# Hybrid encoder block on one core: the rotation of one query pair is moved behind that of the next one, and the key reads with it

## The chip, the core and the metric

The kernel runs on one core of a Trainium2 chip. A core has five engines that run their own instruction streams side by side: TensorE (PE; weight loads are listed apart as PEld), VectorE (DVE), ScalarE (ACT), GpSimd (POOL) and SyncE (SP), which here only issues DMA transfers. ScalarE also issues DMAs, and its DMA instructions stand in the same queue as its arithmetic. Work is handed from one engine to another through semaphores. The two on-chip memories are SBUF (128 partitions) and PSUM, into which matmuls write. The metric is the time of one execution in microseconds (us); less is better.

## The reference

Two inputs, 512 rows and 256 rows of width 2048, go through the same block; the kernel holds them together as 768 rows (`T`), kept transposed as columns. What matters here:

```
h = rmsnorm(x);  z = h @ w_in            # 1024 Fourier | 1024 q | 256 k | 256 v
of = fourier_mix(zf, w_fourier)          # Re(2-D DFT), per-group linear map
q, k = apply_rope(q), apply_rope(k)      # x*cos + rotate_half(x)*sin, head_dim 64
oa = window_attention(q, k, v, sink)     # 16 q heads, 4 kv heads, +-128 positions
x = x + concat(rmsnorm(of), rmsnorm(oa)) @ w_out
x = x + relu(rmsnorm(x) @ w_up)**2 @ w_down;  y = rmsnorm(x)
```

Everything is float32 at the interface. The kernel splits operands into a high part and a remainder in a shorter float format (`wh`/`wl`, `zh`/low part, `ofh`/`ofl`) and adds three products, so each matrix product is three matmuls, and each operand needs one ScalarE instruction (high) and one VectorE instruction (low).

## The kernel before

**Stages.** In order: the v projection, the Fourier columns of `w_in`, then the stage that this change is in: the q and k columns of `w_in` (L802), with the Fourier mix running between its matmuls; then attention together with the Fourier half of `w_out` (L848, L1040); the other half of `w_out`; the up projection; the down projection.

**The q/k stage.** It has 20 pieces (`for piece in range(n_in)`). Four pieces make one *pair*: 256 columns of `w_in`, two channel blocks `c` = 0, 1 of 128, against all 768 rows (two halves `s` of 384). Pair 0 is k; pairs 1 to 4 are the q groups 2, 0, 1 and 3 (`order`). One piece is 48 matmuls: first 24 for `c` = 0, then 24 for `c` = 1. A pair's four PSUM tiles (tag `ps`, four buffers, L802) are complete at the end of its fourth piece. They are then copied to SBUF (L815), block `c` = 0 in the middle of that piece and block `c` = 1 after it. The next pair's matmuls use the same four PSUM buffers, so its first matmul needs the copy of `c` = 0, `s` = 0, and so on.

**Weights.** Each piece's weights come by one 512 KB load into `raw` (two buffers, L79), then `wh` (ACT, L69) and `wl` (DVE, L70). The load of piece p+2 needs the `raw` buffer that piece p gives up when its `wl` is done. Pieces are split two ahead of their matmuls.

**Rotation of a pair.** Rotation works on the tile `zs` (128 x 2 x 768), in three steps of 256 columns: `cross` (POOL, L687: `zy` = the other block times sine), `turned` (DVE, L694 and L696: times cosine, then minus and plus `zy`), `parts` (ACT, L706 or L709: the high part `zh`; DVE, L707 or L710: the low part in place). Each step's parts are written to DRAM by two DMAs that ScalarE issues (L704, 256 KB each: `kh`, `kl` for keys, `qh`, `ql` for queries). Pairs 0 and 1 leave PSUM while the Fourier mix holds the space, so they are put into DRAM as they are and read back by `load_z` (SP, L678). Pairs 2 and 3 are copied from PSUM straight into a `zs` tile of the pool `zo`; pairs 0, 1 and 4 use a `zs` tile of the pool `kp`. Each pool has one buffer of that name. So the copy of pair 3 needs pair 2's writes to be finished, the read-back of pair 1 needs pair 0's, and the copy of pair 4 needs pair 1's.

**Reads for attention.** `load_k` (L720) reads the rotated keys, four DMAs of 768 KB into `kdh` and `kdl`. `load_q` (L731) reads one unit's queries into `qs`, a buffer shared with the `zh` tiles. `load_of` (L188) reads Fourier rows into `ofr`; the first of them use the two `zy` buffers.

**Order.** On TensorE the order is as written. In this stage the other engines' order comes from a scheduler that follows the program order, which the table in the `for pair, t, ahead in ...` loop sets: `after(t, fn)` puts a step behind the first half (t = n - 0.5) or the whole (t = n) of piece n. An engine executes its instructions strictly in that order, so one that waits holds up all behind it. From piece 19 on, the order of SP, ACT, DVE and POOL is as written too. In the attention stage the writing order comes from a list of times, counted in eighths of one output tile (`at(t, fn)`): `t_turn` and `t_parts` place the rotation of pair 4, the last one, `split_of(m)` the high and low parts of row tile m (`ofh`, `ofl`).

Of the kernel before, what the change touches and what calls it, by code (L numbers as in the profile page):

```python
# [11 lines left out]
F32 = mybir.dt.float32  # L12
# [8 lines left out]
P = 128  # L21
# [14 lines left out]
HALF = T // 2  # L36
# [4 lines left out]
def hybrid_encoder(ctx: ExitStack, tc: tile.TileContext, a: dict):  # L41
    nc = tc.nc
    ctx.enter_context(tc.manual_schedule(engines={mybir.EngineType.PE}))

    def f32(ap):
        return ap.bitcast(F32)
# [132 lines left out]
    def load_of(m, tiles=None):  # L179

        of_raw[m] = tiles or [
            op.tile([P, FG, P], F32, tag=f"of{'hl'[m - 1]}-1", name="ofr")
            if m < 3 else ap_.tile([P, FG, P], F32, tag="ofr", name="ofr", bufs=2)
        ]
        for i, raw in enumerate(of_raw[m]):
            k = raw.shape[1]
            src = of_d[i * k * P : (i + 1) * k * P, m * P : (m + 1) * P]
            nc.sync.dma_start(raw[:], src.rearrange("(k p) t -> p k t", p=P))  # L188
# [9 lines left out]
    with ExitStack() as ph:  # L198
# [456 lines left out]
        kt = {}  # L655
# [20 lines left out]
        def load_z(pair):  # L676
            z_tile(pair)
            nc.sync.dma_start(zt[pair][:], zs_d[pair][:].rearrange("(b p) t -> p b t", p=P))  # L678
# [3 lines left out]
        def cross(pair, s):  # L682

            ts = slice(s * 256, (s + 1) * 256)
            y = ys[pair, s] = kt["kp"].tile([P, 2, 256], F32, tag="zy", name="zy", bufs=2)
            for b in range(2):
                nc.gpsimd.tensor_tensor(out=y[:, b], in0=zt[pair][:, 1 - b, ts], in1=kt["sinr"][:, ts], op=ALU.mult)  # L687

        def turned(pair, s):

            ts = slice(s * 256, (s + 1) * 256)
            z, y = zt[pair][:, :, ts], ys.pop((pair, s))
            cb = kt["cosr"][:, ts].rearrange("p (o t) -> p o t", o=1).to_broadcast([P, 2, 256])
            nc.vector.tensor_tensor(out=z, in0=z, in1=cb, op=ALU.mult)  # L694
            for b, op in enumerate((ALU.subtract, ALU.add)):
                nc.vector.tensor_tensor(out=z[:, b], in0=z[:, b], in1=y[:, b], op=op)  # L696

        def parts(pair, s, when=lambda dt, fn: fn()):

            ts = slice(s * 256, (s + 1) * 256)  # L700
            z = zt[pair][:, :, ts]
            out, scale = (kr_d, None) if pair == 0 else (qr_d[order[pair]], HD ** -0.5)
            hi = kt["kp"].tile([P, 2, 256], F32R, tag="zy" if pair == len(cols) - 1 else "qs", name="zh", bufs=2)
            put = lambda o, x: nc.scalar.dma_start(out[o][:, ts].rearrange("(b p) t -> p b t", p=P), x)  # L704
            if scale is None:
                nc.scalar.activation(hi[:], z, AF.Copy)  # L706
                low = lambda: nc.vector.tensor_tensor(out=z.bitcast(F32R), in0=z, in1=f32(hi[:]), op=ALU.subtract)  # L707
            else:
                nc.scalar.activation(hi[:], z, AF.Copy, scale=scale)  # L709
                low = lambda: nc.vector.scalar_tensor_tensor(  # L710
                    out=z.bitcast(F32R), in0=z, scalar=scale, in1=f32(hi[:]), op0=ALU.mult, op1=ALU.subtract
                )
            put(0, f32(hi[:]))
            when(t_zl, low)
            when(t_zp, lambda: put(1, z))
# [9 lines left out]
        def load_q(u):  # L725
            b, g = units[u]
            t0 = slice(b * P, (b + 1) * P)
            qs = kt["kp"].tile([P, 4, P], F32R, tag="qs", name="qs", bufs=2)
            state[u] = {"qs": qs}
            for o in range(2):  # L730
                nc.sync.dma_start(f32(qs[o * HD : (o + 1) * HD]), qr_d[g][o][:, t0].rearrange("(d h) t -> d h t", h=4))  # L731
# [3 lines left out]
        def after(piece, fn):  # L735
            todo.setdefault(piece, []).append(fn)
# [10 lines left out]
        after(10, open_attention)  # L747
        cols = [2048, 1536, 1024, 1280, 1792]
        order = [None, 2, 0, 1, 3]
        for pair, t, ahead in ((0, 10.5, 10), (2, 11.5, None), (1, 13, 12), (3, 15, None)):  # L750
            if ahead is not None:
                after(ahead, lambda pair=pair: load_z(pair))
            for s in range(3):
                after(t + s // 2 * 0.5, lambda pair=pair, s=s: cross(pair, s))
                after(t + 0.5 + s // 2 * 0.5, lambda pair=pair, s=s: (turned(pair, s), parts(pair, s)))
        after(13, load_k)
        for u in range(2):
            after(17 + 0.5 * u, lambda u=u: load_q(u))
        after(17, lambda: load_of(0, [kt["kp"].tile([P, 4, P], F32, tag="zy", name="ofr", bufs=2) for _ in range(2)]))
        n_in = 4 * len(cols)  # L760
        in_raw, in_w = {}, {}

# [25 lines left out]
        for piece in range(n_in):  # L788
            pair, j = divmod(piece, 4)
            if piece == 19:  # L790
                last.enter_context(tc.manual_schedule(engines={mybir.EngineType.SP, mybir.EngineType.Activation, mybir.EngineType.DVE, mybir.EngineType.Pool}))
            if j == 0:
                ps = [[pp.tile([P, 512], F32, tag="ps", bufs=4, name="pz") for _ in range(2)] for _ in range(2)]
            piece_split(piece + 2)
            wh, wl = in_w.pop(piece)
            for c in range(2):
                cs = slice(c * P, (c + 1) * P)
                for i in range(4):
                    first, stop = j == 0 and i == 0, j == 3 and i == 3
                    for w, o, n in ((wh, 0, 0), (wh, 1, 1), (wl, 0, 2)):  # L800
                        for s in range(2):
                            nc.tensor.matmul(  # L802
                                ps[c][s][:, :HALF], w[:, i, cs], whole[j // 2][s][o][:, 4 * (j % 2) + i, :],
                                start=first and n == 0, stop=stop and n == 2,
                            )
                if j == 3:
                    if c == 0 and pair >= 2:
                        z_tile(pair)
                    if pair < 2:
                        zs = fp.tile([P, T], F32, tag="zs", name="zs", bufs=2)  # L810
                        put = [zs[:, :HALF], zs[:, HALF:]]
                    else:
                        put = [zt[pair][:, c, s * HALF : (s + 1) * HALF] for s in range(2)]
                    for s in range(2):
                        (nc.vector.tensor_copy if piece == n_in - 1 and c == 1 else nc.scalar.copy)(put[s], ps[c][s][:, :HALF])  # L815
                    if pair < 2:
                        nc.scalar.dma_start(zs_d[pair][c * P : (c + 1) * P, :], zs[:])
                    if piece == n_in - 1 and c == 0:
                        piece_split(piece + 3)
                if c == 0:  # L820
                    for fn in todo.pop(piece - 0.5, ()):
                        fn()
            for fn in todo.pop(piece, ()):
                fn()
# [159 lines left out]
    pace, t_first, t_qk, d_qk, t_max, t_exp, t_norm = 7.37, 4, -4.5, 1.73, 0.4, 2.65, 3.65  # L984
    t_trans, d_trans, t_th, t_tl, t_pv, d_pv, t_ob, t_os, t_put = 9.2, 1.05, 1.2, 1.4, 16.2, 0, 0.5, -0.6, 2.2
    t_w, t_of, t_xc, t_y, t_oa, t_oa0, t_oa1, t_lq = 42.05, 7.45, -0.05, 2.7, 67, 4.2, 4.95, 1.5
    t_cross, t_turn, t_parts = (0, 0.1, 3.2), (3, 4.6, 6.5), (5.9, 7.6, 9.5)
    t_sq, t_red, t_w3, d_w, t_of1, t_of2, t_lof, t_la = 6.7, 7.9, 1.65, 2.15, 3, 6.5, 15.2, 1
    events, clock = [], [0.0, 0]

    def at(t, fn):
        clock[1] += 1
        heapq.heappush(events, (t, clock[1], fn))
# [9 lines left out]
    for u in range(len(units)):  # L1003
        t = pace * u + t_first
        for h in range(4):
            dt = t_qk + d_qk * h
            at(t + dt, lambda u=u, h=h: qk(u, (h,)))
            at(t + dt + t_max, lambda u=u, h=h: row_max(u, (h,)))
            at(t + dt + t_exp, lambda u=u, h=h: exps(u, (h,)))
        at(t + t_norm, lambda u=u: normalize(u))  # L1010
        if u + 2 < len(units):
            at(t + t_lq + (u == 1), lambda u=u: load_q(u + 2))
        for kb in range(3):
            at(t + t_trans + d_trans * kb, lambda u=u, kb=kb: trans(u, kb))
            at(t + t_pv + d_pv * kb, lambda u=u, kb=kb: pv(u, kb))
# [43 lines left out]
    if True:  # L1059
# [3 lines left out]
        for n in range(4):  # L1063
            for m in range(NM):
                ps = pp3.tile([P, 512], F32, tag="mm", name="pm", bufs=2)
# [586 lines left out]
    ps = [pp.tile([P, 2, 512], F32, tag="ps", name="pd") for _ in range(3)]  # L1652
    ps = [x[:].rearrange("p a b -> p (a b)") for x in ps]
# [27 lines left out]
    for u, (kh, i, j) in enumerate(dunits):  # L1681
        if j == 0 and u > 0:
            ps = [pp.tile([P, 2, 512], F32, tag="ps", name="pd") for _ in range(3)]
            ps = [x[:].rearrange("p a b -> p (a b)") for x in ps]
# [121 lines left out]
```

## Time and profile before

| | |
|---|---|
| median of 3 runs | 2603.39 us (2602.78 to 2604.97) |
| the profiled execution | 2604.47 us |
| its span, first to last instruction | 2602.6 us |
| PE busy in the span | 2579.5 us |
| mean granted TensorE clock | 0.997 |

Stretches of the span, from the times at which the matmuls of a line begin and end: v projection to 57 us, Fourier columns to 173, q/k stage 173.4 to 389.2, attention with the first half of `w_out` from 389.2 to about 610, the rest after that. All times in the rows are from the start of the span. "Landing" of a DMA is the time from its issue to its semaphore. In the chain of waits each row is start, length, what. In a timeline the bracket at a row's end is the engine's idle time before the instruction and what ended it. Rows with PEq, ACTq or SPq are the engine's queue issuing a DMA or waiting.

### The profile page before, as it was taken

The numbers are of one execution on the slowest core, as the hardware profiler recorded it, in microseconds if no ns is written. First come the engines' busy times: TensorE is split into PE (matmuls) and PEld (weight loads), VectorE is DVE, ScalarE is ACT, GpSimd is POOL, SyncE is SP. The second block draws the span as 40 slices with busy tenths as digits, with TensorE's granted clock in tenths as the row PEclk, the third lists the DMA queues.
The fourth block names the chain that finished last, engine by engine and source line by source line (L and its number), as shares of the span: only waits on it lengthen the run. The fifth ranks groups of instructions, "written<-read, shape, count | busy, mean of one in ns | idle before, by whom it ended". The sixth has DMA issues, their size and how long they took to land.

```text
span 2602.6 us, 34971 instructions
## 1 busy us (share of the span) xinstructions
PE 2579.5 (99%) x13580; PEld 2360.6 (91%) x13580; DVE 1808.6 (69%) x2208; ACT 1124.5 (43%) x1574; POOL 264.9 (10%) x367
## 2 busy tenths in 40 slices
PE   9999989999999999999999999999999999999998
PEld 9999987888899999999999999988888888888887
DVE  7966548777556565555777787757776765777687
ACT  6545426675333334333544454433333333333335
POOL 1001323233210011000000000010000000000000
PEclk9999999999999999999999999999999999999999
DMA  7963375345664545466666766685553672554364
GB/s 253 312 221 119 119 217 184 116 127 181 211 207 157 174 162 174 152 206 239 205 213 214 233 232 211 222 319 177 178 164 111 209 244 79 176 183 158 97 210 156
DMA packets 268998, 489.54 MB, mean 188 GB/s; under 512 B 19568, under 2 KB 164000, under 8 KB 267424
## 3 DMA queue, kind: packets, MB, share of 16 engines
q1 hardware_dynamic: 197328, 321.26, 39.0%
q10 hardware_dynamic: 58688, 115.18, 11.7%
q0 software_dynamic: 12816, 50.87, 5.8%
q8 instruction: 107, 1.75, 0.3%
q14 instruction: 59, 0.48, 0.1%
HBM read 360.35 MB, written 126.88 MB: 187 GB/s over the span
## 4 chain that ended last, share of the span: by engine, by line
PE 95%; DVE 2%; DMA 1%; ACT 1%; issue 0%; POOL 0%; ACTq 0%; DVEq 0%; POOLq 0%; SPq 0%
PE pu L1187 35%; PE pd L1622 35%; PE pm L1040 10%; PE pz L802 5%; PE p L268 4%; PE pv L391 1%; PE o L924 1%; PE s L848 1%; PE t L905 1%; DMA raw<-in_w_in 1%; PE pe L630 0%; PE pa L609 0%; PE ptx L137 0%; DMA zs<-zs 0%; POOL zy L687 0%
## 5 line engine op out<-in xcount | busy, mean ns | idle before, releaser
L1187 PE MATMUL pu<-xf,wh 128*128 128x384 f32 x3072 | 780.2, 334 | 0.3
L1187 PEld LDWEIGHTS pu<-xf,wh 128*128 128x128 f32 x3072 | 553.8, 188 | 2.1 <-ACT o L1205 1.7
L1622 PE MATMUL pd<-wh,sh 128*128 128x512 f32 x1332 | 517.7, 389 | 0.0
L1622 PE MATMUL pd<-wl,sh 128*128 128x512 f32 x1332 | 517.7, 389 | 0.0
L1622 PE MATMUL pd<-wh,sl 128*128 128x512 f32 x1332 | 517.5, 389 | 0.0
L1187 PE MATMUL pu<-xf,wl 128*128 128x384 f32 x1536 | 513.1, 334 | 0.0
L1599 ACT ACTIVATE wh<-rd 128x1024 fp32r<-128x1024 f32 x200 | 202.5, 1054 | 522.1 <-PE pd L1622 423.6
L1609 DVE TENSOR_TENSOR wl<-rd,wh 128x1024 fp32r<-128x1024 f32 x200 | 236.1, 1221 | 226.2 <-ACT wh L1599 225.5
L1167 ACT ACTIVATE wh<-ur 128x1024 fp32r<-128x1024 f32 x160 | 170.1, 1063 | 382.6 <-PE pu L1187 211.2
L1622 PEld LDWEIGHTS pd<-wh,sl 128*128 128x128 f32 x1332 | 249.9, 188 | 52.0 <-DVE sl L1610 0.3
L1622 PEld LDWEIGHTS pd<-wh,sh 128*128 128x128 f32 x1332 | 250.0, 188 | 51.9
L1622 PEld LDWEIGHTS pd<-wl,sh 128*128 128x128 f32 x1332 | 250.0, 188 | 51.7
L1187 PEld LDWEIGHTS pu<-xf,wl 128*128 128x128 f32 x1536 | 288.3, 188 | 0.0
L1173 DVE TENSOR_TENSOR wl<-ur,wh 128x1024 fp32r<-128x1024 f32 x160 | 195.4, 1221 | 76.1 <-ACT wh L1167 76.1
L1208 DVE TENSOR_TENSOR o<-pu,o 128x768 f32<-128x768 f32 x160 | 152.8, 956 | 122.4 <-PE pu L1187 114.9
L1592 DVE TENSOR_TENSOR rd<-rd 128x1024 f32<-128x1024 f32 x112 | 131.7, 1217 | 0.0
L1187 PE MATMUL pu<-xs,wh 128*128 128x384 f32 x512 | 129.9, 334 | 0.0
L1167 ACT ACTIVATE wh<-sx 128x1024 fp32r<-128x1024 f32 x64 | 67.9, 1062 | 130.8 <-PE pu L1187 104.6
L268 PE MATMUL p<-xs,wh 128*128 128x384 f32 x448 | 113.7, 334 | 0.0
L1610 DVE TENSOR_TENSOR sl<-sr,sh 128x768 fp32r<-128x768 f32 x111 | 105.5, 951 | 0.0
L1173 DVE TENSOR_TENSOR wl<-sx,wh 128x1024 fp32r<-128x1024 f32 x64 | 78.2, 1222 | 23.8 <-ACT wh L1167 23.6
L70 DVE TENSOR_TENSOR wl<-raw,wh 128x1024 fp32r<-128x1024 f32 x40 | 66.1, 1660 | 40.7 <-ACT wh L69 40.7
(278 smaller groups left out, 3955.8 us busy)
## 6 DMA issues: line engine op xcount, KB each, us to landing
rd<-in_w_down SPq DMA_DIRECT2D x176, 512.0 KB, 5.2
ur<-in_w_up SPq DMA_DIRECT2D x128, 512.0 KB, 4.0
sr<-sd SPq DMA_DIRECT2D x95, 384.0 KB, 5.3
pd<-o ACTq DMA_DIRECT2D x60, 384.0 KB, 2.3
o<-pd POOLq DMA_DIRECT2D x60, 384.0 KB, 6.0
sd<-sm ACTq DMA_DIRECT2D x60, 384.0 KB, 2.8
raw<-in_w_in SPq DMA_DIRECT2D x38, 512.0 KB, 6.2
raw<-in_w_out SPq DMA_DIRECT2D x32, 512.0 KB, 4.8
```

The costliest lines, as they stand in the source:

```text
L268: nc.tensor.matmul(ps7[bank, g, r][:, :HALF], l[:, i, r * P : (r + 1) * P], x[:, o, 4 * e + i, :], start=(opens and e == 0 and i == 0 and ...
L802: nc.tensor.matmul(ps[c][s][:, :HALF], w[:, i, cs], whole[j // 2][s][o][:, 4 * (j % 2) + i, :], start=first and n == 0, stop=stop and n == 2,)
L1040: nc.tensor.matmul(ps, l(k), w[:, k % 2, :], start=(k == 0 and n == 0), stop=(k == 7 and n == 2))
L1167: nc.scalar.activation(wh[:], raw[:], AF.Copy)
L1173: nc.vector.tensor_tensor(out=wl[:], in0=raw[:], in1=f32(wh[:]), op=ALU.subtract)
L1187: nc.tensor.matmul(ps[:, t, :HALF], w[:, i, t * P : (t + 1) * P], xb[:, o, i, :], start=(s == first_of[bank] and i == 0 and n == 0), stop= ...
L1208: nc.vector.tensor_tensor(out=o, in0=src, in1=o, op=ALU.add)
L1592: add = lambda x, y, op: nc.vector.tensor_tensor(out=x[:], in0=x[:], in1=y[:], op=op)
L1599: nc.scalar.activation(wh[:], t[:], AF.Copy)
L1609: nc.vector.tensor_tensor(out=wl[:], in0=t[:], in1=f32(wh[:]), op=ALU.subtract)
L1610: nc.vector.tensor_tensor(out=sl[:], in0=sr[:], in1=f32(sh[:]), op=ALU.subtract)
L1622: nc.tensor.matmul(o, l[:, q, ts], w[:, ns], start=(j == j0 and (q, t) == (0, 0)), stop=(j == j1 and (q, t) == (1, 2)),)
```

## The change

Five numbers or lists of numbers and one condition change. The rotation of pair 1, whose read-back stays behind piece 12, goes from behind piece 13 to behind piece 16.5; that of pair 3, which leaves PSUM after piece 15, stays at 15 and now stands ahead of it. The reads of the keys go from behind piece 13 to behind 14.5, the first two `load_q` and the first `load_of` from 17 to 18. Of the last two PSUM copies of pair 4, one goes from VectorE to ScalarE. The middle step of pair 4's rotation goes behind the low part of row tile 1, the first `parts` a little later with it, and the read of the fourth unit's queries (`load_q(3)`) comes one eighth of a tile later.

```diff
-        for pair, t, ahead in ((0, 10.5, 10), (2, 11.5, None), (1, 13, 12), (3, 15, None)):
+        for pair, t, ahead in ((0, 10.5, 10), (2, 11.5, None), (3, 15, None), (1, 16.5, 12)):
             if ahead is not None:
                 after(ahead, lambda pair=pair: load_z(pair))
             for s in range(3):
                 after(t + s // 2 * 0.5, lambda pair=pair, s=s: cross(pair, s))
                 after(t + 0.5 + s // 2 * 0.5, lambda pair=pair, s=s: (turned(pair, s), parts(pair, s)))
-        after(13, load_k)
+        after(14.5, load_k)
         for u in range(2):
-            after(17 + 0.5 * u, lambda u=u: load_q(u))
-        after(17, lambda: load_of(0, [...]))
+            after(18 + 0.5 * u, lambda u=u: load_q(u))
+        after(18, lambda: load_of(0, [...]))
...
-                        (nc.vector.tensor_copy if piece == n_in - 1 and c == 1 else nc.scalar.copy)(put[s], ps[c][s][:, :HALF])
+                        (nc.vector.tensor_copy if piece == n_in - 1 and c == s == 1 else nc.scalar.copy)(put[s], ps[c][s][:, :HALF])
...
-    t_cross, t_turn, t_parts = (0, 0.1, 3.2), (3, 4.6, 6.5), (5.9, 7.6, 9.5)
+    t_cross, t_turn, t_parts = (0, 0.1, 3.2), (3, 5.2, 6.5), (6.2, 7.6, 9.5)
...
-            at(t + t_lq + (u == 1), lambda u=u: load_q(u + 2))
+            at(t + t_lq + 2 * (u == 1), lambda u=u: load_q(u + 2))
```

No instruction is added or removed, apart from the copy that changes its engine. What moves can be read from the engines' orders. First ScalarE before, from the last write of pair 2 (`ql_83`) on; `qh_86`, `ql_87` are pair 1's parts, and `zs<-pz` are the copies of pair 3 out of PSUM:

```order
L704 DMA ql_83<-zs 128x2x256
L69 ACTIVATE wh<-raw 128x4x4x64
L709 ACTIVATE zh<-zs 128x512
L704 DMA qh_86<-zh 128x2x256
L709 ACTIVATE zh<-zs 128x512
L704 DMA ql_87<-zs 128x2x256
L704 DMA qh_86<-zh 128x2x256
L704 DMA ql_87<-zs 128x2x256
L709 ACTIVATE zh<-zs 128x512
L704 DMA qh_86<-zh 128x2x256
L704 DMA ql_87<-zs 128x2x256
L815 COPY zs<-pz 128x384 x4
```

The same place after the change; `qh_84`, `ql_85` are pair 3's parts:

```order
L704 DMA ql_83<-zs 128x2x256
L69 ACTIVATE wh<-raw 128x4x4x64 x2
L815 COPY zs<-pz 128x384 x2
L69 ACTIVATE wh<-raw 128x4x4x64
L815 COPY zs<-pz 128x384 x2
L709 ACTIVATE zh<-zs 128x512
L704 DMA qh_84<-zh 128x2x256
L709 ACTIVATE zh<-zs 128x512
L704 DMA ql_85<-zs 128x2x256
```

The nine steps of pair 1's rotation have left the place ahead of the copies; in it now stand the weight splits of pieces 18 and 19, the second of them between the two halves of the copies.

Second the DMA queue of SP, as a difference (`zs_79` is the read-back of pair 1, `in_w_in` are the weights of pieces 18 and 19, `in_w_out` the first two of the next stage):

```order
 L720 DMA kdh<-kh 64x3072
 L678 DMA zs<-zs_79 128x2x768
+L79 DMA raw<-in_w_in 128x4x256
 L720 DMA kdh<-kh 64x3072
+L79 DMA raw<-in_w_in 128x4x256
 L720 DMA kdl<-kl 64x3072 x2
-L79 DMA raw<-in_w_in 128x4x256 x2
-L79 DMA raw<-in_w_out 128x2x512
+L79 DMA raw<-in_w_out 128x2x512 x2
 L188 DMA ofr<-ofd 128x4x128
```

Two weight loads pass three of the four key reads, and the second `w_out` load passes an `ofr` load.

Third VectorE at the start of the attention stage, before; L863 and L868 are a row maximum, L694 and L696 the middle step of pair 4's rotation, `ofl_4053` the low part of row tile 1:

```order
L863 ISA p,mx<-s,mask,sink 128x256
L863 ISA mx 128x1
L868 TENSOR_SCALAR nm<-mx 128x1
L694 TENSOR_TENSOR zs<-zs,cosr 128x2x256
L696 TENSOR_TENSOR zs<-zs,zy 128x256 x2
L70 TENSOR_TENSOR ofl_4053<-ofr,ofh_4052 128x1024
```

And after:

```order
L868 TENSOR_SCALAR nm<-mx 128x1
L70 TENSOR_TENSOR ofl_4053<-ofr,ofh_4052 128x1024
L863 ISA p,mx<-s,mask,sink 128x256
L863 ISA mx 128x1
L868 TENSOR_SCALAR nm<-mx 128x1
L870 TENSOR_TENSOR es<-sink,mx 128x4
L694 TENSOR_TENSOR zs<-zs,cosr 128x2x256
L696 TENSOR_TENSOR zs<-zs,zy 128x256 x2
```

Three rotation instructions have gone behind the low part and one more row maximum.

More of the change, by code (lines that the diff above doesn't have):

```diff
@@ L755, in hybrid_encoder @@
                 after(t + 0.5 + s // 2 * 0.5, lambda pair=pair, s=s: (turned(pair, s), parts(pair, s)))
[L756 removed]
+        after(14.5, load_k)
         for u in range(2):
[L758 to L759 removed]
+            after(18 + 0.5 * u, lambda u=u: load_q(u))
+        after(18, lambda: load_of(0, [kt["kp"].tile([P, 4, P], F32, tag="zy", name="ofr", bufs=2) for _ in range(2)]))
         n_in = 4 * len(cols)
```

## The prediction

> **What bounds the kernel now.** I read the page's busy line first:
>
> ```profile
> PE 2579.5 (99%) x13580; PEld 2360.6 (91%) x13580; DVE 1808.6 (69%) x2208; ACT 1124.5 (43%) x1574; POOL 264.9 (10%) x367
> ```
>
> TensorE bounds the kernel: 2579.5 of 2602.6 us busy. A move of instructions on other engines can only win TensorE's idle 23 us, or add to them. So the next view is TensorE's timeline around the change, then the same stretch in windows (us from start to end, PE busy with count, PEld, DVE, ACT, POOL, granted clock, DMA share, GB/s):
>
> ```profile
> 343.81 0.51 PE L802 MATMUL pz<-xs,wl 128*128 128x384 f32 x2
> 353.77 0.69 PE L802 MATMUL pz<-xf,wh 128*128 128x384 f32 x1 [9.45 <-ACT zs L815]
> ...
> 310.88:344.16 33.28, 33.28 (x193) 33.12 (x192) 21.57 (x28) 10.55 (x11) 14.86 (x15) 1.00 0.72 199
> 353.77:389.22 35.45, 35.45 (x192) 35.35 (x193) 14.60 (x17) 12.21 (x16) 7.53 (x6) 0.94 0.67 212
> ...
> 346.00:348.00 2.00, 0.00 (x0) 0.00 (x0) 1.82 (x4) 0.78 (x2) 1.23 (x2) 0.98 0.05 17
> 350.00:353.70 3.70, 0.00 (x0) 0.00 (x0) 1.70 (x4) 1.09 (x3) 0.00 (x0) 0.50 0.92 204
> 356.00:358.00 2.00, 2.00 (x8) 2.00 (x7) 1.37 (x3) 1.54 (x1) 1.14 (x1) 0.50 1.09 377
> ```
>
> Between pieces 15 and 16 TensorE stands still for 9.45 us, waiting for ScalarE's copies. It pays twice: the granted clock falls to 0.50 some 3.6 us into the gap (a mean of 0.98 over 346 to 348 puts the fall at about 347.9) and is still 0.50 at 358, so the 192 matmuls of pieces 16 to 19 take 35.45 us where those of pieces 12 to 15 took 33.28. That is 2.17 us more, and **11.6 us** in all. The chain of waits says why the copies are late, ScalarE's timeline where they stood:
>
> ```profile
> 324.33 7.21 DMA kl<-zs
> 331.60 10.21 DMA zs<-zs
> ...
> 352.78 0.37 ACTq L704
> 353.24 0.49 ACT zs L815
> 353.77 35.45 PE pz L802 x191
> ...
> 335.33 2.04 ACT L69 ACTIVATE wh<-raw 128x1024 fp32r<-128x1024 f32 x1 [2.43 <-issue]
> 353.24 1.63 ACT L815 COPY zs<-pz 128x384 f32<-128x384 f32 x4 [1.22 <-DVE zs L710]
> ```
>
> The copies stand behind pair 1's rotation in ScalarE's queue. That rotation waits for its read-back, issued at 331.60 when pair 0's last write had landed, and landing after 10.21 us. Block `c` = 0 was ready at about 340.2 (half a piece, 4.16 us, before 344.3) and was copied at 353.24.
>
> **The change, part by part.**
>
> *Copies of pair 3 ahead of pair 1's rotation.* This takes away the 11.6 us, if nothing else holds the copies. After it they wait for three things.
>
> First, ScalarE: only the weight split of piece 18 is left ahead of block 0. Its load now follows the read-back, at about 332.0; with the 6.2 us of the page's row it lands at 338.2, with the read-back's 10.2 us at 342.2. I take 339, nearer the row of its own kind, and the split (2.04) ends at 341.
>
> Second, the tile: pair 2's last write must have landed.
>
> ```profile
> raw<-in_w_in SPq DMA_DIRECT2D x38, 512.0 KB, 6.2
> ...
> 333.66 1.57 ACTq L704 DMA_DIRECT2D ql<-zs  x1
> 332.58 15.85 SPq L720 DMA_DIRECT2D kdl<-kl  x2
> SPq L720 <- DMA ql<-zs: 12.8, 1, 12.8
> ...
> kl<-zs ACTq DMA_DIRECT2D x1, 256.0 KB, 2.1
> ```
>
> That write was issued by 335.2 and, by SP's wait of 12.8 us, landed at 348.0; it ran beside two key reads. The `kl` write of the same size took 2.1 us alone and 7.21 us (chain) beside one key read. In the new order one key read is left in front, since the weights of piece 19 now precede the other two. So the ends are 337.3 and 348.0; I take the row with one key read, 342.4. Two copies (0.49 each) end at 343.4, before TensorE needs them at 344.3: cost nothing, cover 0.9 us. [...]
>
> Third, block 1 stands behind the split of piece 19, whose weights are loaded when piece 17's `wl` gives up its buffer.
>
> ```profile
> 337.41 2.01 DVE L70 TENSOR_TENSOR wl<-raw,wh 128x1024 fp32r<-128x1024 f32 x1 [3.78 <-ACT wh L69]
> ...
> raw<-in_w_in SPq DMA_DIRECT2D x1, 512.0 KB, 6.9
> ...
> raw<-in_w_in SPq DMA_DIRECT2D x1, 512.0 KB, 9.1
> ```
>
> Issued at 339.4, landing after 6.2, 6.9 or 9.1 us (the last two are the loads behind key reads), plus 2.04 for the split and 0.49 for the first copy: 348.1, 348.8 or 351.0. TensorE needs block 1 at 344.3 + 4.16 = 348.5. So 0, 0.3 or 2.5 us; I take the row behind one key read, **0.3**.
>
> *Key reads later.* Two weight loads pass them. The last two key reads go out at about 340.5 instead of 332.6 and 348.0; the first use is the end of piece 19, 37 us later, and the read-back of the same size took 10.21. Even one behind the other they are in place with 16 us to spare. Cost nothing.
>
> *Pair 1 last.* Pair 3 now begins after the copies, near 349.4 (339.4 + 6.9 + 2.04 and two copies), and pair 1 follows. The rows are POOL's first steps of pair 1 and of pair 3, the last write, the first query read, the landing of `ql` writes (least, median, most), and VectorE's three kinds of step (ns, least, median, most).
>
> ```profile
> 341.97 3.26 POOL L687 TENSOR_TENSOR zy<-zs,sinr 128x256 f32<-128x256 f32 x4 [14.89 <-DMA zs<-zs]
> 353.85 3.29 POOL L687 TENSOR_TENSOR zy<-zs,sinr 128x256 f32<-128x256 f32 x4 [5.44 <-ACT zs L815]
> 368.26 0.78 ACTq L704 DMA_DIRECT2D ql<-zs  x1
> 368.82 0.56 SPq L731 DMA_DIRECT2D qs<-qh  x1
> DMA to landing us min/median/max: 3.2/5.9/8.7
> ...
> L696 DVE TENSOR_TENSOR zs<-zs,zy x24: 410/418/948, 318.9 to 398.4; 128x256 f32<-128x256 f32 x24
> L694 DVE TENSOR_TENSOR zs<-zs,cosr x11: 677/693/1226, 320.2 to 396.7; 128x512 f32<-128x512 f32 x11
> L710 DVE SCALAR_TENSOR_TENSOR zs<-zs,zh x9: 681/687/693, 328.7 to 367.5; 128x512 fp32r<-128x512 f32 x9
> ```
>
> Pair 1 took 341.97 to 352.78 and 0.37 for its last issue, 11.2 us; pair 3, beside weight splits, 353.85 to 369.0, 15.2 us. One after the other from 349.4 the second ends between 371.8 and 375.8. They overlap, though, as the read-back lands long before: VectorE's share of a pair is three steps of about 2.2 us (0.69 + 2 x 0.42 + 0.69), so the second may end 6.6 us behind the first, at 367.2. I take 367.2, since VectorE carries no weight split in that stretch but one of 1.2 us. The last write lands 5.9 us later (the `ql` row; 3.2 to 8.7), at 373.1. Pair 4's copy needs it at 373.5 at the earliest and SP's `qs` read goes out as before just behind the rotation; attention begins at 377.6 (344.3 + 33.3). Cost nothing; cover 0.4 us before the copies are late, some 4 us before TensorE is.
>
> *Start of attention.* The moved copy stands on ScalarE ahead of `ofh`, and VectorE has one copy of two (1.02) less, 0.5. The first `pm` now waits for a copy and one `ofh` (0.49 + half of 1.15, 1.1 us after the last `pz`) where it began 0.7 after it: 0.4 lost. Then TensorE's weight queue shows the waits of the first 20 us:
>
> ```profile
> 389.25 1.02 DVE L815 COPY zs<-pz 128x384 f32<-128x384 f32 x2 [1.08 <-PE pz L802]
> 386.80 1.15 ACT L69 ACTIVATE ofh<-ofr 128x512 fp32r<-128x512 f32 x2
> 389.95 0.47 PE L1040 MATMUL pm<-wh,ofh 128*128 128x512 f32 x1 [0.33 <-DVE zs L815]
> ...
> 400.04 0.77 PEld L1042 LDWEIGHTS pm<-wh,ofl 128*128 128x128 f32 x4 [1.73 <-DVE ofl L70]
> 403.10 0.19 PEld L848 LDWEIGHTS s<-kdl,qs 128*128 128x128 f32 x1 [0.66 <-DVE mx L863]
> 404.49 0.14 PEld L905 LDWEIGHTS t<-ident,p 128*128 128x128 f32 x1 [0.62 <-POOL p L893]
> ...
> 396.73 0.91 DVE L694 TENSOR_TENSOR zs<-zs,cosr 128x512 f32<-128x512 f32 x1
> 389.00:399.00 10.00, 9.41 (x47) 7.52 (x45) 9.57 (x21) 3.78 (x9) 6.47 (x6) 1.00 0.38 106
> 409.00:419.00 10.00, 9.99 (x53) 8.28 (x52) 8.46 (x29) 8.40 (x23) 3.88 (x7) 1.00 0.68 213
> ```
>
> Moving that step (L694, 0.91, and two L696) behind `ofl` ends the 1.73. But VectorE is busy 9.57 of 10 us there, and the work ahead of the next unit's first maximum shrinks only by the copy and one low part, 0.5 + 0.69, less what `ofl` waits for the later `ofh`. So the next wait grows, and of 1.73 some 0.6 is won; then the transposes wait for `p`, whose exponentials stand on ScalarE behind a `zh` that now waits for the moved step. What is late next is `p`, at about the same time as before. Ends: 0.5 lost, 1.0 won; I take **0**. From 409 on TensorE is full, so an earlier start is kept.
>
> **Sum.** 9.45 + 2.17 - 0.3 - 0 = 11.3 us off the profiled execution: span 2602.6 to 2591.3, time 2604.47 to 2593.2. That execution is 1.1 us above the median of the runs, 2603.39; off the median it gives **2592.1 us**.
>
> **Rivals.**
>
> *The copies get a new wait* (0.24). If pair 2's last write still lands at 348.0, block 0 is copied by 348.5 and TensorE idles 4.2 us. The clock fell after 3.6 us of idling, so most of the 2.17 us would be paid too: 11.6 - 4.2 - 2.1 = 5.3 won, 2598.1. With the late weights of piece 19 instead, 2.5 us idle and no fall: 9.1 won, 2594.3. For it: the 12.8 us wait. Against it: the reads that caused it are behind. [...]
>
> *Slower: pair 1 is late for pair 4* (0.08). Both use the `kp` buffer, and pair 1 is now the last rotation before the copy that overwrites it. Behind that copy on ScalarE stand a weight split, another copy and `ofh`, some 3.1 us, before the first `pm`, which came at 389.95. It breaks even when the last write lands at 386.9, and is slower by 0.2% (5.2 us) from 392.1. The slowest rows, 375.8 + 8.7, give 384.5 and about 2601. For it: a cover of 0.4 us. Against it: 19 us to the point of loss.
>
> *The start of attention gives it back* (0.06). If VectorE's backlog of the first 20 us costs what its waits show (1.73 + 0.66) once more, 2594.5.
>
> **How the numbers follow.** The forecast has 0.62, with 2590.6 to 2593.9 as its own range (from 1.0 won at attention and no wait, to 0.5 lost there and a wait of 1.6). About 0.2% or 5 us is what a measurement tells from no change; faster means below 2598.2. Forecast, third rival and nearly all of the first give 0.90 faster; the first's tail and the middle of the second 0.06 same; the rest 0.04 slower. The range runs from 2590.4 to 2597.2, so that the tail of the first rival and the second are left out.
>
> **What would show it.** Right: no gap of TensorE over 1 us at L815 between pieces 15 and 16, a clock of 1.00 through pieces 16 to 19, their 192 matmuls in 33.3 us, the first `pm` near 378.5. The first rival shows as a gap named after ScalarE's copies with a DMA before them, the second as copies of pair 4 waiting for `ql`. I am wrong if a queue that I moved past holds longer than its rows: SP issuing three loads in a row at 332, or the third write of pair 2.

## The result: faster by 8.6 us, and where the time went

| | before | after |
|---|---|---|
| median of 11 runs each | 2604.13 us (2602.41 to 2607.35) | 2595.83 us (2594.31 to 2598.56) |
| the profiled execution | 2604.47 us, span 2602.6 | 2594.31 us, span 2592.3 |
| mean granted TensorE clock | 0.997 | 0.999 |

After to before is 0.9967, with a 95% interval of 0.9958 to 0.9976: 8.6 us won, 6.2 to 10.9; the medians themselves stand 8.3 us apart. The forecast was 11.3 us won and 2592.1 us, with 2590.6 to 2593.9 as its own range: 2595.83 lies above that, inside the whole range of 2590.4 to 2597.2. The two profiled executions stand 10.2 us apart; the one of after is the shortest of its eleven.

First TensorE's timeline of after between pieces 15 and 16, then the windows (us from start to end, PE with count, PEld, DVE, ACT, POOL, granted clock, DMA share, GB/s), the same stretches as before the change where they have an equal:

```profile
343.93 0.51 PE L802 MATMUL pz<-xs,wl 128*128 128x384 f32 x2
345.21 1.17 PE L802 MATMUL pz<-xf,wh 128*128 128x384 f32 x4 [0.77 <-ACT zs L815]
```

```profile
345.21:378.81 33.60, 33.60 (x192) 33.40 (x193) 20.61 (x28) 10.69 (x15) 12.03 (x12) 1.00 0.77 233
346.00:348.00 2.00, 2.00 (x14) 2.00 (x13) 0.00 (x0) 1.64 (x1) 0.02 (x1) 1.00 0.97 197
350.00:353.70 3.70, 3.70 (x24) 3.70 (x23) 2.45 (x4) 0.00 (x0) 2.89 (x3) 1.00 0.89 213
...
394.00:402.00 8.00, 7.64 (x31) 6.05 (x32) 5.13 (x19) 5.81 (x15) 1.68 (x5) 0.79 0.91 287
```

The gap of 9.45 us is 0.77 us, the clock stays at 1.00, and the 192 matmuls of pieces 16 to 19 take 33.60 us instead of 35.45. That is 8.68 + 1.85 = 10.5 us. The last row shows something new: at the start of attention the clock falls (a mean of 0.79 over 394 to 402), to which the experiments come back.

What is left of the gap, in after's chain of waits and in ScalarE's timeline:

```profile
329.20 5.28 DMA qh<-zh
...
334.55 0.64 ACT zh L709
...
335.22 0.70 DVE zs L710
...
335.94 8.67 DMA ql<-zs
...
344.68 0.49 ACT zs L815
...
345.21 33.60 PE pz L802 x191
```

```profile
340.45 2.05 ACT L69 ACTIVATE wh<-raw 128x1024 fp32r<-128x1024 f32 x1 [2.00 <-DMA raw<-in_w_in]
344.68 0.86 ACT L815 COPY zs<-pz 128x384 f32<-128x384 f32 x2 [2.18 <-DMA ql<-zs]
346.36 2.04 ACT L69 ACTIVATE wh<-raw 128x1024 fp32r<-128x1024 f32 x1 [0.82 <-DMA raw<-in_w_in]
348.19 0.90 ACT L815 COPY zs<-pz 128x384 f32<-128x384 f32 x2
...
375.05 0.86 ACT L815 COPY zs<-pz 128x384 f32<-128x384 f32 x2 [2.34 <-DMA ql<-zs]
378.84 0.48 ACT L815 COPY zs<-pz 128x384 f32<-128x384 f32 x1 [1.97 <-PE pz L802]
```

In this profile block `c` = 0 of pair 3 waits for one thing only, pair 2's last write, which lands after 8.67 us. The copies of pair 4 at 375.05 wait for pair 1's last write. At the start of attention TensorE's waits are these (window 290 to 440 us: in total, times, longest):

```profile
PE t L905 <- POOL p L893: 1.1, 1, 1.1
PE pz L802 <- ACT zs L815: 0.8, 1, 0.8
PE pm L1040 <- ACT ofh L69: 0.7, 1, 0.7
PE s L848 <- DVE mx L863: 0.6, 1, 0.6
```

One way of splitting a profile serves all that follows: the end of the last `pz`, from there to the first matmul of the up projection (`pu`, L1187), and the rest of the span. Before and after, the last `pz` row and the first `pu` row of TensorE's timeline:

```profile
388.88 0.51 PE L802 MATMUL pz<-xs,wl 128*128 128x384 f32 x2
745.67 0.51 PE L1187 MATMUL pu<-xf,wh 128*128 128x384 f32 x2
```

```profile
378.46 0.51 PE L802 MATMUL pz<-xs,wl 128*128 128x384 f32 x2
736.09 0.51 PE L1187 MATMUL pu<-xf,wh 128*128 128x384 f32 x2
```

So to the end of `pz` 389.39 became 378.97 (10.4 us won), from there to `pu` 356.28 became 357.12 (0.8 us lost), and the rest 1856.9 became 1856.2. No instruction of the rest was moved, so that the 0.7 us there has no place in the change; over all fourteen profiles it lies between 1856.2 and 1857.1, the same to 0.03 us in two or three profiles of one kernel, and no run here says why it differs from kernel to kernel.

### The profile page after: what moved, and what is told of

Its sections match the earlier page's. It is cut to its first block, busy times and chain, and to the rows that moved or that the text cites. A ratio compares the mean times of both kernels' runs of the same rounds, so it can differ in the third digit from the quotient of the medians.

```text
span 2592.3 us, 34971 instructions
## 1 busy us (share of the span) xinstructions
PE 2577.8 (99%) x13580; PEld 2359.7 (91%) x13580; DVE 1809.2 (70%) x2207; ACT 1124.6 (43%) x1575; POOL 263.3 (10%) x367
## 4 chain that ended last, share of the span: by engine, by line
PE 96%; DVE 1%; DMA 1%; POOL 0%; ACT 0%; issue 0%; DVEq 0%; POOLq 0%; SPq 0%; ACTq 0%
PE pu L1187 36%; PE pd L1622 35%; PE pm L1040 10%; PE pz L802 5%; PE p L268 5%; PE pv L391 1%; PE o L924 1%; PE t L905 1%; PE s L848 1%; DMA raw<-in_w_in 1%; PE pe L630 0%; PE pa L609 0%; PE ptx L137 0%; DMA ql<-zs 0%; PE pt L137 0%; POOL zy L687 0%
## 5 line engine op out<-in xcount | busy, mean ns | idle before, releaser
L1187 PE MATMUL pu<-xf,wh 128*128 128x384 f32 x3072 | 780.1, 334 | 0.0
L1187 PEld LDWEIGHTS pu<-xf,wh 128*128 128x128 f32 x3072 | 554.0, 188 | 1.5 <-ACT o L1205 1.3
L1187 PE MATMUL pu<-xf,wl 128*128 128x384 f32 x1536 | 513.1, 334 | 0.0
L1187 PEld LDWEIGHTS pu<-xf,wl 128*128 128x128 f32 x1536 | 288.3, 188 | 0.0
L1187 PE MATMUL pu<-xs,wh 128*128 128x384 f32 x512 | 129.8, 334 | 0.0
L101 POOL TENSOR_TENSOR ry<-ry,mhalf 128x1 f32<-128x1 f32 x5 | 5.5, 1097 | 871.6 <-DVE ry L98 871.6
```

Of the source, the lines that this page charges most:

```text
L1187: nc.tensor.matmul(ps[:, t, :HALF], w[:, i, t * P : (t + 1) * P], xb[:, o, i, :], start=(s == first_of[bank] and i == 0 and n == 0), stop= ...
```

## The experiments

The theory under test: the copies of pair 3 were late for their place behind pair 1's rotation on ScalarE, and the key reads beside pair 2's last write set what is left; the edits at the start of attention sum to nothing. The times of before that the ratios use were taken beside each group of runs: 2603.49 us for the order alone, the key reads alone and the first runs without and with only the attention edits; 2603.78 for the changed kernel's first repeat, the key reads behind the weight loads and the copy back; 2604.28 for the rest.

### The order alone

```diff
-        for pair, t, ahead in (..., (1, 13, 12), (3, 15, None)):
+        for pair, t, ahead in (..., (3, 15, None), (1, 16.5, 12)):
-            after(17 + 0.5 * u, lambda u=u: load_q(u))
+            after(18 + 0.5 * u, lambda u=u: load_q(u))
-        after(17, lambda: load_of(0, ...))
+        after(18, lambda: load_of(0, ...))
```

> The kernel before with the order of the rotations changed (pair 3 ahead of pair 1, the first query and Fourier reads behind piece 18) and the key reads left behind piece 13. Theory: the place of the copies behind pair 1's rotation made the 9.45 us gap, and the key reads in front of them set only what is left of it. The copies stand free of pair 1, but pair 2's last write again runs beside several key reads and lands near 348, so TensorE waits some 4 us at L815 (3 to 5), the clock may still fall for a part of the next pieces, and 5 to 7.5 us are won against before: 2596.5 to 2599. Rival A, that the key reads alone were the cause: the gap stays near 9 us and nothing is won. Rival B, that the place alone was the cause and the key reads cost nothing: the gap is under 1 us and all of the 8 to 10 us are won.

2603.22 us (2601.12 to 2605.42), ratio 0.9996 (0.9987 to 1.0005): nothing won. Its profile, the shortest of its runs, in TensorE's timeline, the chain of waits and a window:

```profile
350.10 1.71 PE L802 MATMUL pz<-xf,wh 128*128 128x384 f32 x4 [5.48 <-ACT zs L815]
```

```profile
334.40 15.10 DMA ql<-zs
...
349.56 0.49 ACT zs L815
```

```profile
350.10:385.86 35.76, 35.76 (x194) 35.67 (x194) 22.51 (x30) 14.13 (x19) 12.78 (x12) 0.93 0.66 201
```

The copies are free of pair 1's rotation and wait all the same: pair 2's last write, beside three key reads, takes 15.10 us. The clock falls (a mean of 0.93 over the 35.76 us, 1.00 in after), and the matmuls of pieces 16 to 19 cost as much more as before the change (35.60 us by the chain, 35.45 before). Expected were 5 to 7.5 us; even this shortest run is only 3.4 us below before's profiled one, and the median 0.3. A run at the median has no profile, so where the other 3 us go is not shown. Rival B, that the place alone was the cause, falls. The later query and Fourier reads were not tried apart from the order.

### The key reads alone

```diff
-        after(13, load_k)
+        after(14.5, load_k)
```

> The kernel before with the key reads moved behind piece 14.5 and nothing else. Theory: the copies still stand behind pair 1's rotation on ScalarE; its read-back and writes come somewhat earlier beside fewer key reads, so the gap before piece 16 stays, 6 to 9.5 us, the clock falls as before, and 0 to 3 us are won (2601 to 2604). Rival A (the key reads are the cause): the gap goes to under 2 us and 8 us or more are won. Rival B (the place alone): no change, the gap within 1 us of 9.45.

2604.86 us (2602.85 to 2606.87), ratio 1.0004 (0.9995 to 1.0013). The gap, and ScalarE's first and third `zh` of pair 1:

```profile
354.24 1.70 PE L802 MATMUL pz<-xf,wh 128*128 128x384 f32 x4 [9.28 <-ACT zs L815]
```

```profile
343.57 0.63 ACT L709 ACTIVATE zh<-zs 128x512 fp32r<-128x512 f32 x1 [6.60 <-DVE zs L696]
...
351.32 0.63 ACT L709 ACTIVATE zh<-zs 128x512 fp32r<-128x512 f32 x1 [5.91 <-DMA qh<-zh]
```

Pair 1's rotation begins 3.1 us earlier than before (343.57 against 346.65) and its third `zh` comes at the same time (351.32 against 351.39), since it waits 5.91 us for a `qh` write: the key reads, later, meet the writes of the rotation that still stands ahead of the copies. Rival A falls. Neither of the two parts wins anything, and both together 8 to 10 us: each removes one of two holds on the same copies, and the one that is left is nearly as long. By the profiles the copies began at 353.24 before, at 349.56 with the order alone, at 353.67 with the key reads alone, and at 344.68 with both.

### Without the edits at the start of attention

```diff
-  (... n_in - 1 and c == s == 1 else nc.scalar.copy)
+  (... n_in - 1 and c == 1 else nc.scalar.copy)
-  t_turn, t_parts = (3, 5.2, 6.5), (6.2, 7.6, 9.5)
+  t_turn, t_parts = (3, 4.6, 6.5), (5.9, 7.6, 9.5)
-  at(t + t_lq + 2 * (u == 1), lambda u=u: load_q(u + 2))
+  at(t + t_lq + (u == 1), lambda u=u: load_q(u + 2))
```

(against the changed kernel)

> The changed kernel without the edits at the start of attention: the last copy back on VectorE, the middle step of pair 4's rotation and the fourth query read back at their old places. Theory: these edits sum to nothing (0.5 lost to 1.0 won), so the time is within 1 us of the changed kernel's (2595 to 2597), and 7.5 to 9 us better than before. Rival C: a good part of the gain comes from the start of attention, then 2 us or more are lost against the changed kernel (over 2598).

2594.0 us of 5 runs (2593.17 to 2596.99), ratio 0.9964 (0.9952 to 0.9977). All of the gain is there. The same kernel again, later, beside the changed one:

> The kernel without the edits at the start of attention once more, since its first median (2594.0, of five runs) stood 1.8 us below the changed kernel's. Theory (the edits sum to nothing, 1.7 us at half clock against a wait of 1.3 us for ofl and shorter others): within 0.8 us of the changed kernel beside it, clock 1.00 where the changed kernel has the fall. Rival: they cost 1 us or more.

2594.28 us (2592.97 to 2594.77), ratio 0.9960 (0.9947 to 0.9972); the changed kernel beside it had 2594.6. The edits bring no gain that can be told from none.

### The edits at the start of attention alone

The same three edits the other way round, put into the kernel before.

> The kernel before with only the edits at the start of attention: one of the last two copies on ScalarE, the middle step of pair 4's rotation behind the low part of row tile 1, the fourth query read one eighth of a tile later. Theory: within 1 us of before (2603 to 2605), the gap before piece 16 unchanged at 9 to 9.5 us. In the trace the first pm comes 1.1 us after the last pz where it came 0.7 after it, and the weight queue's wait of 1.7 us for the low part ofl is gone or under 0.7, with longer waits for p behind it. Rival C: 2 us or more won.

2603.87 us (2602.5 to 2607.03), ratio 1.0003 (0.9994 to 1.0011): nothing, as expected. TensorE's waits in its profile:

```profile
PE pz L802 <- ACT zs L815: 6.7, 1, 6.7
PE t L905 <- POOL p L893: 1.0, 1, 1.0
...
```

The wait of 1.3 us for `ofl` is gone, and 1.0 for `p` has come, with 0.7 for `ofh` and 0.6 for `mx` as in the changed kernel. The gap here is 6.7 us in a kernel whose q/k stage is that of before, where 9.45 us were profiled, though 9 to 9.5 were expected: its length differs from run to run.

### The changed kernel again, twice

> The changed kernel once more, for a second profile of it. In the first one pair 2's last write took 8.67 us and left a wait of 0.8 us at L815, in a run that was the fastest of its eleven. If the landing of that write is what differs from run to run, this profile has a wait between 0.3 and 3 us there, and its time is longer or shorter by the same amount; if not, the wait is 0.8 within 0.3 us whatever the time.

> The changed kernel a third time, beside the three runs that follow. All profiles so far of kernels with the edits at the start of attention have a granted clock of 0.50 from about 16 to 20 us after the last pz (0.79 in the 8 us window that holds it), and none without them has. Theory: this one has it again, and a time of 2594 to 2597. Rival: it comes and goes from run to run, then the clock is 1.00 there.

2595.34 us (2593.64 to 2596.49), ratio 0.9968 (0.9956 to 0.9980), and 2594.6 us (2593.61 to 2596.01), ratio 0.9963 (0.9950 to 0.9975). In the first, profiled at 2593.64, TensorE has no wait at L815. In the second, profiled at 2596.01, it has this one (timeline, then the chain):

```profile
346.16 1.18 PE L802 MATMUL pz<-xf,wh 128*128 128x384 f32 x4 [1.46 <-ACT zs L815]
```

```profile
335.97 9.60 DMA ql<-zs
```

So the wait at L815 is 0, 0.77 or 1.46 us in three profiles of one kernel, and their times follow the end of their last `pz` (378.33, 378.97, 380.37) at a distance of 2215.3 to 2215.6 us. The write is hardly shorter in the first, where it was issued at 334.30 and the copies that waited for it began at 343.85 (9.5 us); it was issued 1.6 us earlier. In the second ScalarE waited 5.0 us for the load of piece 18 (2.00 in after), which by after's rows puts the end of its split at about 345.5, as late as the write (345.57); so a faster write alone would have won next to nothing there. The first profiled execution, with a time 1.5 us below its median, thus flattered the change: if the distance holds, a run at the median has its last `pz` near 380.4. The fall of the clock at the start of attention, to 0.50, is in both, 3.4 us long.

### All key reads behind the weight loads

In the changed kernel the load for piece 18 passes three key reads and that for piece 19 two. Here SP's order is taken as written from piece 14 on, so that all four key reads stand behind both loads and one of the next stage.

```diff
-        after(14.5, load_k)
+        after(15.5, load_k)
-            if piece == 19:
-                last.enter_context(tc.manual_schedule(engines={mybir.EngineType.SP, mybir.EngineType.Activation, mybir.EngineType.DVE, mybir.EngineType.Pool}))
+            if piece in (14, 19):
+                last.enter_context(tc.manual_schedule(engines={mybir.EngineType.SP} if piece == 14 else {mybir.EngineType.SP, mybir.EngineType.Activation, mybir.EngineType.DVE, mybir.EngineType.Pool}))
```

> The changed kernel with all four key reads behind both weight loads and one load of the next stage (SP's order written out from piece 14 on, the reads behind piece 15.5). Theory: pair 2's last write then runs beside no key read from about 335 on but for the one issued at 325, lands by 340 to 341, the copies of pair 3 wait for nothing but the matmuls, TensorE's wait of 0.8 us at L815 goes, the clock stays, and 0.5 to 1.5 us are won against the changed kernel (2594 to 2595.5). Rival: the write is slow for another reason than the key reads (the weight load and the read-back beside it), lands at 344 again, and nothing is won.

> The kernel of the run before (all key reads behind the weight loads) without the edits at the start of attention. Both edits together, if each is worth what the other runs say: 0.5 to 1.5 us for the key reads and 0 to 2 us for leaving the attention edits out, 2592 to 2595. Rival: the 1.8 us between the medians with and without the attention edits was scatter, then within 0.7 us of the run before.

2595.38 us (2594.26 to 2598.65), ratio 0.9970 (0.9958 to 0.9981), and 2595.42 us (2593.72 to 2597.08), ratio 0.9968 (0.9956 to 0.9981): no gain over the changed kernel. ScalarE's timeline of the second, and TensorE's waits of the first from 344 to 420 us:

```profile
336.24 0.66 ACTq L704 DMA_DIRECT2D ql<-zs  x1
337.00 2.05 ACT L69 ACTIVATE wh<-raw 128x1024 fp32r<-128x1024 f32 x1 [1.52 <-PE pz L802]
339.23 2.06 ACT L69 ACTIVATE wh<-raw 128x1024 fp32r<-128x1024 f32 x1 [0.17 <-DMA raw<-in_w_in]
341.09 0.89 ACT L815 COPY zs<-pz 128x384 f32<-128x384 f32 x2
```

```profile
...
PE s L848 <- DMA qs<-ql: 0.8, 1, 0.8
PE pm L1040 <- DVE wl L70: 0.8, 1, 0.8
...
```

The write does what the theory says: without key reads beside it pair 2's last write, issued at 336.24, is there by 341.09 (at most 4.9 us), and TensorE waits at L815 in neither profile. The rival is not wholly excluded, since the read-back moves away from the write too: it was issued 7.3 us ahead of the write here and 7.8 in the other profile, in after 2.0. Against the read-back as the cause stands the order alone, where it was issued 2.1 us ahead and the write took 15.10 us, not 8.67.

The reads now run where the first queries and weights of attention are loaded. A new wait for `wl` is in both profiles (0.8 and 0.6 us) and one for `qs` in the first. From the last `pz` to the first `pu` the two take 361.5 and 358.3 us where the changed kernel takes 357.1 to 357.5. The 361.5 overstate it: that profile is the longest run of its six, 3.3 us above their median, and has 6.8 us of half clock. That these waits are what takes back the gain is likely from these rows but not shown apart.

### The last copy back on VectorE

The first line of the three edits alone, taken back in the changed kernel.

> The changed kernel with the last copy out of PSUM back on VectorE, so that ScalarE begins with ofh. Theory (0.4 us of the start of attention is lost to the copy ahead of ofh): the first pm comes 0.3 to 0.8 us after the last pz where it came 1.1 after it, but VectorE has 0.5 us more to do before its first low part, so that the weight queue's later waits grow by about as much: the time is within 0.7 us of the changed kernel's. Rival: the copy's place decides, and 1 us or more is won.

2595.3 us (2594.15 to 2597.59), ratio 0.9970 (0.9958 to 0.9981), the changed kernel beside it 2595.34. The first `pm` comes 0.6 us after the last `pz` and not 0.9, and nothing is won: the copy's place does not decide.

### The high part behind the exponential

In the six profiles of kernels that have the attention edits as they stand (the changed one three times, with the copy moved back, with the key reads behind, and the edits alone) the clock falls to 0.50 in the first 25 us of attention, for 3.4 us (twice, 6.8 us, in the one with the key reads behind); in the six without the edits (before among them) it never does. The trace of after says what is late there: the fourth exponential of the first unit (`p`, L878) runs on ScalarE at 391.78, behind a `zh` that waits for the moved step, though its maximum was there at 388.5. The next kernel puts that `zh` behind it:

```diff
-    t_turn, t_parts = (3, 5.2, 6.5), (6.2, 7.6, 9.5)
+    t_turn, t_parts = (3, 5.2, 6.5), (7.4, 7.6, 9.5)
```

> The changed kernel with the first high part of pair 4's rotation (zh, with its write) on ScalarE behind the fourth exponential of the first unit, not ahead of it. Theory: in the changed kernel that exponential is ready at 388.5 and runs at 391.78, behind zh, which waits for the moved middle step; so the wait of 1.05 us for p goes, and with it the fall of the clock (3.4 us at half speed, 1.7 us): 1.5 to 2.8 us won against the changed kernel, 2592.5 to 2594.5. Rival: p is late for VectorE's sake (the sum and its reciprocal behind a low part), then the wait and the clock stay and the time is within 0.7 us.

2593.93 us (2593.1 to 2595.45), ratio 0.9961 (0.9948 to 0.9973), 0.7 us below the changed kernel beside it (2594.6), which these runs can't tell from nothing. ScalarE, VectorE, TensorE's waits and a window:

```profile
388.17 0.51 ACT L878 ACTIVATE p<-p,nm 128x256 f32<-128x256 f32 x1 [0.78 <-DVE nm L868]
```

```profile
390.91 0.47 DVE L863 CUSTOM_DVE_ANT_0 p<-s,mask,sink 128x256 f32<-128x256 f32 x1
...
391.69 0.18 DVE L891 RECIPROCAL rs<-rs 128x4 f32<-128x4 f32 x1
```

```profile
PE s L848 <- DVE mx L863: 1.2, 2, 0.7
PE t L905 <- POOL p L893: 0.7, 1, 0.7
PE pm L1040 <- ACT ofh L69: 0.3, 1, 0.3
...
```

```profile
394.00:402.00 8.00, 7.30 (x37) 5.69 (x37) 6.18 (x20) 6.50 (x17) 2.29 (x6) 1.00 0.86 269
```

The exponential runs 3.6 us earlier, and the fall of the clock is gone. `p` still waits 0.7 us, now for the reciprocal, which stands on VectorE behind two rotation steps and a maximum. From the last `pz` to the first `pu` it takes 356.4 us, 0.8 less than the changed kernel, where 1.5 to 2.8 were expected; the rest of the span, where nothing moved, is 0.9 us longer (1857.1), so the time shows nothing of it. VectorE's queue is the next to be late: behind the last `pz` TensorE's waits are 2.2 us in total here and 2.4 in the changed kernel. Why the 1.7 us that 3.4 us of half clock would cost (an estimate, 3.4 x 0.5) are not won on top is not shown. It is the best median of the study with the one without the attention edits (2594.0 and 2594.28), and neither can be told from the changed kernel.

### The last step behind the reciprocal too

```diff
-    t_turn, t_parts = (3, 5.2, 6.5), (7.4, 7.6, 9.5)
+    t_turn, t_parts = (3, 5.2, 7.8), (7.4, 7.6, 9.5)
```

> The kernel of the run before with the last step of pair 4's rotation on VectorE behind the next unit's first row maximum and the reciprocal as well. Theory: the wait of 0.59 us for mx goes too and p comes earlier still, so 0.3 to 0.8 us beside the run before: 2 to 3.5 us won against the changed kernel, 2592 to 2594. Rival: the last step, moved, makes a low part or a later exponential late, and nothing is won beside the run before, or up to 1 us lost.

2597.86 us of 8 runs (2595.21 to 2599.05), ratio 0.9974 (0.9964 to 0.9985): slower than all its neighbours. From the last `pz` to the first `pu` it takes 357.1 us, 0.7 us more than the kernel before it, and the clock falls again (0.79 from 394 to 402). But most of the 4 us stand earlier, where no instruction was moved: ScalarE waits for the weight loads of pieces 18 and 19.

```profile
344.55 2.00 ACT L69 ACTIVATE wh<-raw 128x1024 fp32r<-128x1024 f32 x1 [6.92 <-DMA raw<-in_w_in]
...
350.06 2.04 ACT L69 ACTIVATE wh<-raw 128x1024 fp32r<-128x1024 f32 x1 [2.81 <-DMA raw<-in_w_in]
```

These loads landed some 10 us after their issue (339.71 to 350.06 for the second), and TensorE waited 1.80 and 0.89 us at L815. Why they are slow in this kernel is open; nothing ahead of them differs in the instructions, and only one of the eight runs has a profile, though the median says that most are late. It also sets a bound for this study: two kernels that are alike up to there can stand 3 us apart.

## Why the prediction was right, and by how much

**What bounds it.** Right. Both costs, the gap and the clock's fall, were where the forecast saw them, and of the 11.6 us 10.5 went in the profiled pair. Of the signs that the prediction gave, the clock of 1.00 through pieces 16 to 19 is there; the wait at L815 is under 1 us in two of three profiles; the matmuls took 33.60 us for 33.3, and the first `pm` came at 379.90 for 378.5.

**The wait for the tile.** The term that was mis-sized. Pair 2's last write was given 7.21 us and 0.9 us of cover; it was issued at 335.94, not by 335.2, and took 8.67 us, and the copies came 0.8 us late: 0.77 instead of 0. It lies inside the bounds given (337.3 to 348.0), and with 9.60 us in another run it is a wait of 1.46. What the two queues sent beside each other differs from stretch to stretch. From 340 to 342 us in after SP's queue sent 34 packets (0.42 MB, some 12 KB each) and ScalarE's 34 (0.03 MB, some 1 KB each), from 336 to 338 us 314 (0.74 MB) and 3; in before, beside two key reads, it was 33 (0.33 MB) and 87 (0.09 MB) from 342 to 344 us. No run here gives the reason.

**The two weight splits.** The split of piece 18 ended at 342.5, not 341, and hid behind the write; with the key read it is the next in line, as the second of the two later profiles of the changed kernel (about 345.5) and the last kernel (346.6) show. The split of piece 19 ended at 348.4 in time; the 0.3 us were not paid. In that second one they were: ScalarE waited 1.9 us for the load and not 0.82, and from the first matmul of piece 16 to the last `pz` it took 34.21 us, where after took 33.76.

**Key reads later.** Costing nothing was right at the place chosen. But it priced the reads too low as a cause: with pair 2's write still beside them (the first rival) 5.3 us were to be won, and the order alone, which is that case, won 0.3 by its median and 3.4 by its profile.

**Pair 1 last.** Its last write was issued at 371.24, some 4 us after the 367.2 forecast and before the 371.8 of no overlap (the overlap of the two rotations was taken too large). Pair 4's copies started at 375.05 and not at 373.5, after a wait of 2.34 us for `ql`, the sign given for the second rival. TensorE lost nothing by it: the cover of some 4 us held. The point at which it costs was not tried.

**Start of attention.** Net 0 was forecast, from 0.5 lost to 1.0 won; from the last `pz` to the first `pu` it is 0.8 lost, in the edits alone (357.11) as in the changed kernel (357.12, before 356.28). That this is the edits' work is not shown, since the kernels without them that have the new order stand at 357.0 to 357.4 as well. The steps were right (a later `ofh`, `ofl` in time, then `mx` and `p` late behind a `zh` that waits for the moved step); what was missed is that the clock falls there (to 0.50, for 3.4 us) with no wait of TensorE over 1.05 us.

**The sum.** Off the span, 10.3 us against 11.3. To the end of `pz`: 0.77 less for the write and 0.32 less because the 192 matmuls took 33.60 and not 33.28, the first four of them 1.17 us instead of 0.85, 0.3 more for the split that was not paid, and 0.1 less from stages ahead. Behind it 0.8 lost to the first `pu` and 0.7 won in the rest; that these two nearly cancel is luck, since the change moved nothing in the rest. The medians fall further short, 8.3 us against 11.3: before's profiled run stands 0.3 above the median of its eleven and after's 1.5 below its own, so the pair shows 1.9 us more than the medians. The last 0.7 us between 2592.1 and 2595.83 are the base, 2603.39 by three runs and 2604.13 by eleven. (The forecast's own lower end, from the terms that it names, would be 2590.8 and not 2590.6.) The rival *the copies get a new wait* came true in a small form, with 0.8 us of its 4.2 in the first profile; the other two did not come.

## What to carry to other kernels

The copies waited behind two things that ended at about the same time: each edit alone showed no gain (ratios 0.9996 and 1.0004), both together 0.9967, and dropping either as useless would have lost both. So before pricing a move, list all that must be over for the late instruction, each with its own end. A large read that nothing needs for 30 us belongs behind the small write that holds up the bottleneck (here the write took 15.10 us beside three such reads and 8.67 beside one), but not so far behind that it meets the next stage's first loads (here 361.5 and 358.3 us from the last `pz` to the first `pu`, where the changed kernel had 357.1 to 357.5). And a time of one profiled run is compared with the median of its own runs first.

## What the runs showed of the hardware

- A 256 KB write from ScalarE's queue took 15.10 us with three 768 KB reads of SyncE's queue issued within 2 us of it (the order alone), 12.8 with two (before), 8.67 and 9.60 with one (the changed kernel in two profiles; in after the other two followed 5 us behind it), and at most 4.9 with none, where the read-back had been issued 7.3 us ahead of it and not 2.0. It landed within 1 us of the last of those reads in before (348.0 and 347.2) and in after (344.61 and 343.7).
- The granted clock fell to 0.50 in after at about 395 us, though no wait of TensorE around it was longer than 1.05 us: from 391 to 395 it was busy 2.1 of 4 us, by windows of 1 us (0.41, 1.00, 0.06, 0.66). It then stayed low for 3.4 us, and this length came back in each kernel that had the fall (3.40 to 3.42, or 6.82), added up from such windows; the fall ahead of piece 16 lasted 10.24 us before.
- What the fall of the clock cost pieces 16 to 19 did not grow with the length of the gap ahead of them, in four profiles: by the chain of waits they took 35.60 us after a gap of 5.48, 35.38 after 6.68, 35.62 after 9.28 and 35.45 after 9.45, against 33.60 after 0.77.
